# A hybrid decoder layer on one core: the output gate made token-major, two pooling maps to a PSUM bank, token-major weight tiles by high part first, and a norm's columns scaled ahead of its transposes

## The chip, the core and the metric

The kernel runs on one core of one Trainium2 chip. The metric is device time in microseconds (us), from launch to end, of one execution. The core has five engines that run side by side and meet only at semaphores: TensorE (PE; its weight loads are shown apart as PEld), VectorE (DVE), ScalarE (ACT), GpSimd (POOL), and SyncE (SP), which issues most DMAs. PE writes its results to PSUM, which this kernel uses as eight banks of 512 fp32 columns, four of them (`acc`) for the projections; DVE and ACT carry them on to SBUF.

## The reference, cut to what matters

256 tokens of width 2048 pass through one layer. All matrices are fp32.

```
proj = h @ w_in                      # 2048 x 5136: q, k, v, z, b, a, p
o = chunk_gated_delta_rule(q, k, v, g, beta)           # 8 heads x 128
o = o * rsqrt(mean(o*o) + eps) * norm_w                # per head
o_gdn = o * silu(z)                                    # the output gate
pooled = window_means(p) - p                           # 4 groups x 256 channels
o_pool = einsum("btgc,gcd->btgd", pooled, pool_w) * pool_scale   # the pooling maps
h = LN1(ALPHA*h + concat(o_gdn, o_pool) @ w_out)
h = LN2(ALPHA*h + cross_attention(h, mem))             # wq, wk, wv, wo: 2048 x 2048
h = LN3(ALPHA*h + square(relu(h @ w_up)) @ w_down)     # 2048 x 8192, 8192 x 2048
```

## The kernel before, in words

**Products in three parts.** Each fp32 operand is split into a high part (rounded to fp32r by ACT, line 189) and a low part (the difference, by DVE, line 190). A product is the sum of high x high, high x low and low x high. A weight matrix comes in tiles of 256 rows by 512 columns (`W`, 512 KB); the split makes `H` and `L` of each, three buffers of either, so a tile is split two or three tiles ahead of its matmuls.

**Two ways to lay out a projection.** `proj_a` puts out features on the partitions: the weight block is the stationary operand and the tokens stream. In its `wide` form a matmul of 512 columns (line 328) streams the high and the low part of the tokens side by side against a high weight block, and one of 256 columns (line 332) streams the high part against the low block; the two halves of the result are added later (`fold`: ACT copies the bank, line 201, POOL adds the halves, line 204). A tile takes 8 of each. `proj_b` puts out tokens on the partitions (token-major): the tokens are stationary and the weights stream, 512 columns at a time, by three matmuls per row block and token block (`one`, lines 374 to 376: high.H, high.L, low.H). A tile takes 12. `proj_b` serves w_out, w_v, w_o and w_down.

**The order of the work.** The list `plan` holds every weight tile in order, and `run` walks it: it issues the DMAs and the splits of the tiles ahead, then the tile's matmuls, then one step of the background scheduler `bg`. Background tasks (the delta rule, the gate, the pooling, the attention, the norms) are generators; each `yield` names the DVE and ACT time that it spent and how many tiles to wait. `bg.step` takes from them until a slot's budget is spent. So the order on each engine is fixed when the program is built, and each engine runs its queue in that order.

**The places that the change touches.** w_in's tiles for z are projected by wide `proj_a`; `z_evac` folds each head's block and a later step applies SiLU to 128x256 (line 934). `solve` ends by scaling the delta rule's output by its norm (line 916); `gate_out` transposes a head (line 944), multiplies by norm_w and the gate on DVE (line 946) and splits the result. `pool_map` makes a group of four maps: for each, six matmuls of 256 columns (lines 1003 to 1005) into a bank of its own (`acc()` hands out four banks in turn), an ACT eviction with the scale (line 1009) and a DVE eviction of the low part (line 1010). The group stands as one tile in the plan, once inside and once behind w_k's tiles. The second norm works on two token blocks, `norm0` and `norm1`. `Norm.start` centers and scales columns on DVE (lines 1105 and 1110) and hands two groups of 512 columns to ACT and POOL (`beside`); `Norm.turn` transposes blocks on PE (line 1311) and stores them by ACT and DVE (lines 1134 and 1136). The dictionaries `after_o` and `after_up` say behind which tile of w_o and of the first w_up tiles each step stands. The first w_up tiles are walked twice, for either token block (lines 1377 to 1379).

Of the kernel before, what the change touches and what calls it, by code (L numbers as in the profile page):

```python
# [15 lines left out]
P = 128  # L16
T = 256
# [107 lines left out]
def hybrid_layer(ctx: ExitStack, tc: tile.TileContext, xT, xtok, memT, w_ba, w_in, small, w_pool,  # L125
# [19 lines left out]
    def chunk(shape, dtype=F32, late=False):  # L145
        pool = second[0] if late else cp
        return pool.tile([P] + list(shape), dtype, tag="c", name=nm("c"))
# [44 lines left out]
    def pair():  # L192
        a = chunk([2, T], F32R)
        r = Pair((a[:, 0, :], a[:, 1, :]))
        r.wide = a.rearrange("p s c -> p (s c)")
        return r
# [170 lines left out]
    def proj_b(src, acts, evac, resident=False, pre=None, post=None):  # L367
# [3 lines left out]
        def one(t, kt, h, l):  # L371
            a = acts[kt]
            c = slice(t * P, (t + 1) * P)
            mm(out=accs[t], lhsT=a[0][:, c], rhs=h, start=kt == 0, stop=False)  # L374
            mm(out=accs[t], lhsT=a[0][:, c], rhs=l, start=False, stop=False)  # L375
            mm(out=accs[t], lhsT=a[1][:, c], rhs=h, start=False, stop=kt == KT - 1)  # L376
            if kt == KT - 1:
                evac(t, accs[t])

        def both(j):  # L380
            def fn(h, l):
                if j == 0:
                    accs.extend(acc() for _ in range(NT))
                for t in range(NT):
                    for s in range(2):
                        one(t, 2 * j + s, h[:, s, :], l[:, s, :])
            return fn

        def first(j):
# [447 lines left out]
    def solve(g):  # L837
# [73 lines left out]
        r = small_tile([NT, 4])  # L911
        rsqrt(r, ms, [NT, 4])
        yield 1.2, 1.5, 0
        for a in range(NT):
            for i in range(4):
                V.tensor_scalar(out=os_[a][:, i, :], in0=os_[a][:, i, :], scalar1=r[:, a, i:i + 1],
                                scalar2=None, op0=ALU.mult)
                yield .2, 0, 0
        og[g] = os_

    zsil = [None] * 4

    def z_evac(g):
        def evac(n, o):
            h = 4 * g + n
            if h % 2 == 0:
                zsil[h // 2] = chunk([2, T])
            bg.urgent.append(silu(h, fold(o, zsil[h // 2][:, h % 2, :])))
        return evac

    def silu(h, z):
        yield 0, 0, 1
        yield 0, 0, 1
        S.activation(out=z, in_=z, func=AF.Silu)
        bg.event(f"z{h}")
        yield 0, .35, 0

    def gate_out(h):
        g, n = h // 4, h % 4
        zs = zsil[h // 2][:, h % 2, :]  # L940
        yield from free_aux()
        ps = aux()
        for a in range(NT):
            nc.tensor.transpose(out=ps[:, a * P:(a + 1) * P], in_=og[g][a][:, n, :], identity=ident)
        yield 0, 0, 1
        V.scalar_tensor_tensor(out=zs, in0=ps[:, :T], scalar=par[:, C_NW:C_NW + 1], in1=zs,
                               op0=ALU.mult, op1=ALU.mult)
        done()
        yield .4, 0, 1
        mix[8 + h] = pair()  # L950
        split(*mix[8 + h], zs)
        yield .35, .3, 0

    pooled = [None] * 8
    raw_p = {}
# [37 lines left out]
    def pool_map(g):  # L993

        def fn(h, l):
            for gi in range(2):
                for nb in range(2):
                    ps = acc()
                    o = ps[:, :T]
                    for s in range(2):  # L1000
                        a = pooled[4 * g + 2 * gi + s]
                        c = slice(nb * P, (nb + 1) * P)
                        mm(out=o, lhsT=h[:, gi, s, c], rhs=a[0], start=s == 0, stop=False)
                        mm(out=o, lhsT=h[:, gi, s, c], rhs=a[1], start=False, stop=False)
                        mm(out=o, lhsT=l[:, gi, s, c], rhs=a[0], start=False, stop=s == 1)
                    b = 4 * g + 2 * gi + nb
                    m = pair()
                    sc = par[:, C_PS + b:C_PS + b + 1]
                    S.activation(out=m[0], in_=o, func=AF.Copy, scale=sc)
                    V.scalar_tensor_tensor(out=m[1], in0=o, scalar=sc, in1=m[0].bitcast(F32),  # L1010
                                           op0=ALU.mult, op1=ALU.subtract)
                    mix[b] = m
        add("w", w_pool[g], [2, 2, 256], fn, [f"pool{4 * g + i}" for i in range(4)])
# [13 lines left out]
    for g in range(2):  # L1027
        bg.add(f"solve{g}", solve(g), *[f"v{4 * g + i}" for i in range(4)], *[f"diag{q}" for q in range(4)])
    for h in range(HEADS):
        bg.add(f"gate{h}", gate_out(h), f"solve{h // 4}", f"z{h}")  # L1030
    for h in range(HEADS):
        bg.add(f"q{h}", q_head(h), f"x{8 + h}", f"k{h}")
    for h in range(HEADS):
# [5 lines left out]
            t[2] += tuple(f"q{4 * int(t[0][5:]) + i}" for i in range(4))  # L1039
    for i in range(2, 6):  # L1040
        proj_a(w_in[i], xs, conv_evac(4 * i, True), wide=True)
    proj_a(w_in[6], xs, z_evac(0), wide=True)
    proj_a(w_in[7], xs, z_evac(1), wide=True)
    proj_a(w_in[8], xs, p_evac(0), wide=True)
    proj_a(w_in[9], xs, p_evac(1), wide=True)

# [273 lines left out]
    def steps(*fs):  # L1320
# [9 lines left out]
        11: steps((norm0.turn, 0, 1)),  # L1330
        13: steps((norm0.turn, 2, 3)),
        14: steps((norm0.turn, 4, 5)),
        15: steps((norm1.start, 5, [half0, half1, (1, ALL)], [half0, half1], (2, 3))),
    }
    after_up = {
        2: steps((norm1.turn, 0, 1), (norm1.scale, (1, ALL))),
        J: steps((norm1.turn, 2, 3)),
        J + 1: steps((norm0.turn, 6, 7)),
        J + 2: steps((norm1.turn, 4, 5)),
# [241 lines left out]
```

## Time and profile before

| | |
|---|---|
| median of 3 runs | 1483.5 us (1483.07 to 1484.04) |
| the profiled execution | 1483.14 us, of it span 1481.3 us |
| PE busy | 1472.4 us, 99% of the span |
| DVE busy | 943.4 us, 64% |
| ACT busy | 728.2 us, 49% |
| POOL busy | 148.8 us, 10% |
| DMA | 280.45 MB, mean 189 GB/s |

The span runs from the first instruction to the last; 1.8 us lie around it. PE's busy time counts overlapping matmuls: one of 512 columns is shown as 390 ns or so from start to end, while the next may start some 230 ns after it. So the pace of PE is read from starts, not from durations.

### The profile page before, as it was taken

How to read it: one execution, taken by the hardware profiler on the slowest of the kernel's cores; microseconds unless marked ns; L12 is line 12 of the kernel's file. 1: busy time of each engine (PE TensorE's matmuls, PEld its weight loads, DVE VectorE, ACT ScalarE, POOL GpSimd, SP SyncE). 2: the span in 40 equal slices, each digit the busy share in tenths (PEclk: the TensorE clock that was granted, in tenths of full speed). 3: DMA queues.
4: the chain of work that ended last, by engine and by line, in shares of the span. 5: the costliest groups of instructions: out<-in, count | busy, mean ns of one | idle time of the engine just before them, and what ended most of it. 6: DMA issues, size and time to landing. Idle time of an engine off the chain costs nothing.

```text
span 1481.3 us, 21143 instructions
## 1 busy us (share of the span) xinstructions
PE 1472.4 (99%) x8050; PEld 1277.3 (86%) x8050; DVE 943.4 (64%) x1464; ACT 728.2 (49%) x1064; POOL 148.8 (10%) x191
## 2 busy tenths in 40 slices
PE   9999999999999999999999999999999999999998
PEld 9988889899888888998888888888888888888887
DVE  6778976867656755555685555566545565556557
ACT  6765555755533545453545443355344453345442
POOL 1024323700300000000130000000000000000001
PEclk9999999999999999999999999999999999999999
DMA  8556565535865555444735655555656655555562
GB/s 274 182 203 185 171 187 173 194 130 170 288 197 189 183 190 190 155 133 159 276 131 178 199 191 190 196 187 183 198 190 212 222 192 194 196 190 185 194 233 83
DMA packets 86902, 280.45 MB, mean 189 GB/s; under 512 B 13920, under 2 KB 15216, under 8 KB 86800
## 3 DMA queue, kind: packets, MB, share of 16 engines
q1 hardware_dynamic: 79072, 268.73, 54.7%
q0 software_dynamic: 2960, 9.58, 2.0%
q10 hardware_dynamic: 4768, 0.79, 0.3%
q8 instruction: 63, 1.03, 0.3%
q14 instruction: 39, 0.32, 0.1%
HBM read 276.43 MB, written 2.63 MB: 188 GB/s over the span
## 4 chain that ended last, share of the span: by engine, by line
PE 98%; DVE 1%; ACT 0%; issue 0%; DMA 0%; DVEq 0%; ACTq 0%
PE acc L328 30%; PE acc L332 15%; PE acc L374 13%; PE acc L376 13%; PE acc L375 13%; PE acc L349 5%; PE acc L411 0%; PE acc L410 0%; PE acc L409 0%; PE acc L1377 0%; PE acc L1379 0%; PE acc L1378 0%; PE aux L1224 0%; PE aux L1223 0%; PE aux L855 0%
## 5 line engine op out<-in xcount | busy, mean ns | idle before, releaser
L190 DVE TENSOR_TENSOR L<-W,H 128x1024 fp32r<-128x1024 f32 x469 | 578.1, 1234 | 462.2 <-ACT H L189 456.6
L189 ACT ACTIVATE H<-W 128x1024 fp32r<-128x1024 f32 x479 | 507.4, 1059 | 582.7 <-PE acc L376 298.7
L328 PE MATMUL acc<-c,H 128*128 128x512 f32 x1920 | 499.2, 394 | 0.0
L328 PEld LDWEIGHTS acc<-c,H 128*128 128x128 f32 x1920 | 338.3, 189 | 55.3 <-DVE c L190 0.6
L374 PE MATMUL acc<-H,c 128*128 128x512 f32 x832 | 325.2, 391 | 0.0
L376 PE MATMUL acc<-H,c 128*128 128x512 f32 x832 | 323.9, 389 | 0.0
L375 PE MATMUL acc<-L,c 128*128 128x512 f32 x832 | 323.9, 389 | 0.0
L332 PEld LDWEIGHTS acc<-c,L 128*128 128x128 f32 x1920 | 274.2, 190 | 27.2
L332 PE MATMUL acc<-c,L 128*128 128x256 f32 x1920 | 281.3, 282 | 0.0
L376 PEld LDWEIGHTS acc<-H,c 128*128 128x128 f32 x832 | 156.2, 188 | 32.6
L375 PEld LDWEIGHTS acc<-L,c 128*128 128x128 f32 x832 | 156.3, 188 | 31.7
L374 PEld LDWEIGHTS acc<-H,c 128*128 128x128 f32 x832 | 156.2, 188 | 31.7
L204 POOL TENSOR_TENSOR c<-c 128x256 f32<-128x256 f32 x60 | 49.8, 855 | 369.9 <-DVE L L190 186.6
L190 DVE TENSOR_TENSOR c<-c,c 128x256 fp32r<-128x256 f32 (+1 forms) x170 | 76.6, 503 | 11.4 <-ACT c L189 11.4
L189 ACT ACTIVATE c<-c 128x256 fp32r<-128x256 f32 (+1 forms) x170 | 66.6, 456 | 4.6 <-DMA c<-xT 4.6
L349 PE MATMUL acc<-c,H 128*128 128x256 f32 x384 | 66.7, 290 | 0.7 <-ACT H L189 0.7
L1095 POOL DMA_DIRECT2D c<-lnrow x24 | 12.9, 539 | 517.8 <-PE acc L376 345.0
L349 PEld LDWEIGHTS acc<-c,H 128*128 128x128 f32 x384 | 58.2, 198 | 1.6 <-ACT H L189 1.4
L349 PE MATMUL acc<-c,L 128*128 128x256 f32 x192 | 48.0, 289 | 0.0
L201 ACT ACTIVATE c<-acc 128x512 f32<-128x512 f32 x60 | 35.6, 599 | 18.9 <-PE acc L332 14.9
L566 DVE SCALAR_TENSOR_TENSOR c<-c,par 128x255 f32<-128x255 f32 (+2 forms) x72 | 38.2, 538 | 3.6 <-ACT c L563 1.9
L349 PEld LDWEIGHTS acc<-c,L 128*128 128x128 f32 x192 | 34.4, 197 | 0.2 <-DVE L L190 0.2
(258 smaller groups left out, 1000.8 us busy)
## 6 DMA issues: line engine op xcount, KB each, us to landing
W<-w_up SPq DMA_DIRECT2D x127, 512.0 KB, 4.2
W<-w_down SPq DMA_DIRECT2D x120, 512.0 KB, 4.3
W<-w_in SPq DMA_DIRECT2D x76, 512.0 KB, 3.4
W<-w_k SPq DMA_DIRECT2D x32, 512.0 KB, 3.4
W<-w_out SPq DMA_DIRECT2D x32, 512.0 KB, 4.3
W<-w_v SPq DMA_DIRECT2D x32, 512.0 KB, 3.3
W<-w_q SPq DMA_DIRECT2D x32, 512.0 KB, 3.3
W<-w_o SPq DMA_DIRECT2D x24, 512.0 KB, 3.5
```

What stands on the lines that cost most here:

```text
L189: S.activation(out=h, in_=src, func=AF.Copy)
L190: eng.tensor_tensor(out=l, in0=src, in1=h.bitcast(F32), op=ALU.subtract)
L201: S.activation(out=ab.rearrange("p s c -> p (s c)"), in_=o, func=AF.Copy)
L204: nc.gpsimd.tensor_tensor(out=r, in0=ab[:, 0, :], in1=ab[:, 1, :], op=ALU.add)
L328: mm(out=accs[n], lhsT=h[:, s, c], rhs=acts[k0 + s].wide, start=k0 + s == 0, stop=False)
L332: mm(out=accs[n][:, :T], lhsT=l[:, s, c], rhs=acts[k0 + s][0], start=False, stop=k0 + s == KT - 1)
L349: mm(out=accs[n][:, :T], lhsT=w[:, s, n * P:(n + 1) * P], rhs=acts[kt][x], start=kt == 0 and w is h and x == 0, stop=kt == KT - 1 and w is l)
L374: mm(out=accs[t], lhsT=a[0][:, c], rhs=h, start=kt == 0, stop=False)
L375: mm(out=accs[t], lhsT=a[0][:, c], rhs=l, start=False, stop=False)
L376: mm(out=accs[t], lhsT=a[1][:, c], rhs=h, start=False, stop=kt == KT - 1)
L566: V.scalar_tensor_tensor(out=u[:, sh:], in0=x[:, :T - sh], scalar=w[:, 3 - sh:4 - sh], in1=u[:, sh:], op0=ALU.mult, op1=ALU.add)
L1095: nc.gpsimd.dma_start(out=c, in_=lnrow[i:i + 1, g * 512:(g + 1) * 512].partition_broadcast(P))
```

## The change: what it does

Five edits:

1. z's two groups of w_in tiles go through `proj_b`: 12 matmuls of 512 columns per tile. The result stands token-major in a full bank, and one ACT instruction per token block takes it through SiLU. The folds of z fall away.
2. `solve` multiplies by the norm and by the gate in one DVE instruction; `gate_out` only transposes, and evicts the high and the low part straight from PSUM.
3. `proj_b`'s `both` no longer calls `one`: a tile runs all high.H, then all low.H, then all high.L, across both token blocks; in the last tile of a group, block by block.
4. `pool_map` takes one bank for two maps, a half each.
5. `norm1`'s scaling of column group 1 moves from `after_up[2]`, behind the first transposes, to the end of `after_o[15]`, ahead of them.

```
 def both(j): ...
-                for t in range(NT):
-                    for s in range(2):
-                        one(t, 2 * j + s, h[:, s, :], l[:, s, :])
+                last = 2 * j + 2 == KT
+
+                for ts in [[t] for t in range(NT)] if last else [range(NT)]:
+                    for x, w in ((0, h), (1, h), (0, l)):
+                        for t in ts:
+                            for s in range(2):
+                                kt = 2 * j + s
+                                mm(out=accs[t], lhsT=acts[kt][x][:, t * P:(t + 1) * P], rhs=w[:, s, :],
+                                   start=kt == 0 and x == 0 and w is h, stop=kt == KT - 1 and w is l)
+                    if last:
+                        evac(ts[0], accs[ts[0]])
...
+        while f"z{g}" not in bg.done:
+            yield 0, 0, 1
         for a in range(NT):
             for i in range(4):
-                V.tensor_scalar(out=os_[a][:, i, :], in0=os_[a][:, i, :], scalar1=r[:, a, i:i + 1],
-                                scalar2=None, op0=ALU.mult)
+                V.scalar_tensor_tensor(out=os_[a][:, i, :], in0=os_[a][:, i, :], scalar=r[:, a, i:i + 1],
+                                       in1=four(zsil[g][a])[:, i, :], op0=ALU.mult, op1=ALU.mult)
...
     def z_evac(g):
...
+        def evac(t, o):
+            zsil[g][t] = chunk([512])
+            S.activation(out=zsil[g][t], in_=o, func=AF.Silu)
...
     def gate_out(h):
...
-        V.scalar_tensor_tensor(out=zs, in0=ps[:, :T], scalar=par[:, C_NW:C_NW + 1], in1=zs,
-                               op0=ALU.mult, op1=ALU.mult)
+        mix[8 + h] = m = pair()
+        sc = par[:, C_NW:C_NW + 1]
+        S.activation(out=m[0], in_=ps[:, :T], func=AF.Copy, scale=sc)
+        V.scalar_tensor_tensor(out=m[1], in0=ps[:, :T], scalar=sc, in1=m[0].bitcast(F32), op0=ALU.mult,
+                               op1=ALU.subtract)
         done()
-        yield .4, 0, 1
-        mix[8 + h] = pair()
-        split(*mix[8 + h], zs)
-        yield .35, .3, 0
...
     def pool_map(g): ...
             for gi in range(2):
+                ps = acc()
                 for nb in range(2):
-                    ps = acc()
-                    o = ps[:, :T]
+                    o = ps[:, nb * T:(nb + 1) * T]
...
-    proj_a(w_in[6], xs, z_evac(0), wide=True)
-    proj_a(w_in[7], xs, z_evac(1), wide=True)
+    proj_b(w_in[6], xs, z_evac(0))
+    proj_b(w_in[7], xs, z_evac(1))
...
-        15: steps((norm1.start, 5, [half0, half1, (1, ALL)], [half0, half1], (2, 3))),
+        15: steps((norm1.start, 5, [half0, half1, (1, ALL)], [half0, half1], (2, 3)), (norm1.scale, (1, ALL))),
     }
     after_up = {
-        2: steps((norm1.turn, 0, 1), (norm1.scale, (1, ALL))),
+        2: steps((norm1.turn, 0, 1)),
```

How the instructions stand on the engines, at three places.

PE, the first two maps of the first `pool_map`, before (`H` and `L` are the split map weights, `c` the pooled tokens, `acc` the bank; in brackets the engine whose semaphore a row waits for):

```order
L1003 MATMUL acc_3986<-c_3483,H_3911 128x256 [waits Activation_49]
L1004 MATMUL acc_3986<-c_3483,H_3911 128x256
L1005 MATMUL acc_3986<-c_3483,L_3912 128x256
L1003 MATMUL acc_3986<-c_3526,H_3911 128x256
L1004 MATMUL acc_3986<-c_3526,H_3911 128x256
L1005 MATMUL acc_3986<-c_3526,L_3912 128x256
L1003 MATMUL acc_3996<-c_3483,H_3911 128x256 [waits Activation_49]
L1004 MATMUL acc_3996<-c_3483,H_3911 128x256
```

The same place in the change:

```order
L1008 MATMUL acc_3915<-c_3264,H_3826 128x256 [waits Activation_49]
L1009 MATMUL acc_3915<-c_3264,H_3826 128x256
L1010 MATMUL acc_3915<-c_3264,L_3827 128x256 [waits DVE_49]
L1008 MATMUL acc_3915<-c_3419,H_3826 128x256
L1009 MATMUL acc_3915<-c_3419,H_3826 128x256
L1010 MATMUL acc_3915<-c_3419,L_3827 128x256
L1008 MATMUL acc_3915<-c_3264,H_3826 128x256 [waits DVE_49]
L1009 MATMUL acc_3915<-c_3264,H_3826 128x256
```

The second map now writes the bank of the first (`acc_3915`), and its first matmul waits for a DVE semaphore, where it waited for an ACT semaphore before a bank of its own (`acc_3996`); its operands are those that the first map has already read. The third and fourth map, and the second `pool_map`, stand in the same way.

PE, the first tile of z, the change (`H` and `L` of the weights now stream, `c` holds the tokens; before, this was 8 rows of line 328 over four banks and 8 of line 332):

```order
L391 MATMUL acc_1960<-H_1884,c_143 128x512 [waits Activation_49]
L391 MATMUL acc_1960<-H_1884,c_154 128x512
L391 MATMUL acc_1961<-H_1884,c_143 128x512 [waits Activation_49]
L391 MATMUL acc_1961<-H_1884,c_154 128x512
L391 MATMUL acc_1960<-H_1884,c_143 128x512
L391 MATMUL acc_1960<-H_1884,c_154 128x512
L391 MATMUL acc_1961<-H_1884,c_143 128x512
L391 MATMUL acc_1961<-H_1884,c_154 128x512
L391 MATMUL acc_1960<-L_1885,c_143 128x512 [waits Pool_49]
L391 MATMUL acc_1960<-L_1885,c_154 128x512
L391 MATMUL acc_1961<-L_1885,c_143 128x512
L391 MATMUL acc_1961<-L_1885,c_154 128x512
```

This is also the new order of every token-major tile: the four matmuls that read `L` come last, and the bank changes at every second matmul instead of at every sixth.

DVE, the start of `norm1`, before (`c_4474` is column group 1, line 1110 the scaling, line 1136 the store of transposed blocks):

```order
L1110 SCALAR_TENSOR_TENSOR c_4470<-c_4470,t_7883,c_7609 128x256
L1121 SCALAR_TENSOR_TENSOR t_7888<-t_7870,t_7883 128x1
L1136 TENSOR_TENSOR c_7763<-aux_7915,c_7763 128x128 [waits Activation_49]
L1136 TENSOR_TENSOR c_7764<-aux_7915,c_7764 128x128
L1136 TENSOR_TENSOR c_7769<-aux_7918,c_7769 128x128 [waits Activation_49]
L1136 TENSOR_TENSOR c_7770<-aux_7918,c_7770 128x128
L1110 SCALAR_TENSOR_TENSOR c_4474<-c_4474,t_7883,c_7611 128x512
```

and in the change (the lines are 5 higher):

```order
L1115 SCALAR_TENSOR_TENSOR c_4338<-c_4338,t_7775,c_7501 128x256
L1126 SCALAR_TENSOR_TENSOR t_7780<-t_7762,t_7775 128x1
L1115 SCALAR_TENSOR_TENSOR c_4342<-c_4342,t_7775,c_7503 128x512
L1141 TENSOR_TENSOR c_7655<-aux_7808,c_7655 128x128 [waits Activation_49]
L1141 TENSOR_TENSOR c_7656<-aux_7808,c_7656 128x128
L1141 TENSOR_TENSOR c_7661<-aux_7811,c_7661 128x128 [waits Activation_49]
L1141 TENSOR_TENSOR c_7662<-aux_7811,c_7662 128x128
```

The scaling of 512 columns has moved ahead of four stores that wait for ACT.

## Rows read from the trace of the kernel before

**Rows 1.** The page: PE's busy time, and its granted clock in 40 slices.

```profile
PE 1472.4 (99%) x8050; PEld 1277.3 (86%) x8050; DVE 943.4 (64%) x1464; ACT 728.2 (49%) x1064; POOL 148.8 (10%) x191
...
PEclk9999999999999999999999999999999999999999
```

**Rows 2.** Waits of PE: who waited for whom, total us, times, longest.

```profile
PE aux L464 <- DVE warm L426: 1.5, 1, 1.5
PE aux L1506 <- DVE c L1504: 1.2, 1, 1.2
PE aux L1311 <- DVE c L1110: 0.7, 1, 0.7
```

**Rows 3.** Timeline of PE, a wide z tile: start us, us, line, operation, tiles.

```profile
157.58 2.00 PE L328 MATMUL acc<-c,H 128*128 128x512 f32 x8
...
160.37 2.00 PE L328 MATMUL acc<-c,H 128*128 128x512 f32 x8
```

**Rows 4.** The same tile from 158.5 us on, a closer window.

```profile
158.51 1.07 PE L328 MATMUL acc<-c,H 128*128 128x512 f32 x4
159.42 0.40 PE L332 MATMUL acc<-c,L 128*128 128x256 f32 x2
```

**Rows 5.** The chain that ended last, in w_down: start us, us, what.

```profile
1040.14 0.23 PE acc L374
...
1055.78 0.23 PE acc L374
```

**Rows 6.** Busy time by stretch (us, busy per engine, granted clock, DMA).

```profile
157.58:205.65 48.07, 48.07 (x283) 42.36 (x281) 42.62 (x70) 23.95 (x35) 13.27 (x9) 1.00 0.55 175
...
1470.00:1476.00 6.00, 4.79 (x20) 2.71 (x19) 4.07 (x12) 0.90 (x2) 1.14 (x2) 1.00 0.22 68
```

**Rows 7.** Groups of instructions: the folds' additions on POOL.

```profile
L204 POOL TENSOR_TENSOR c<-c 128x256 f32<-128x256 f32 x60 | 49.8, 855 | 369.9 <-DVE L L190 186.6
```

**Rows 8.** Timeline around the first pool_map: ACT, DVE, and PE at the second map.

```profile
345.22 2.69 ACT L201 ACTIVATE c<-acc 128x512 f32<-128x512 f32 x4 [1.43 <-PE acc L332]
...
347.83 0.28 PE L1003 MATMUL acc<-c,H 128*128 128x256 f32 x1
...
348.28 1.06 ACT L189 ACTIVATE H<-W 128x1024 fp32r<-128x1024 f32 x1
...
349.23 1.57 ACT L1009 ACTIVATE c<-acc,par 128x256 fp32r<-128x256 f32 x4
...
349.37 1.23 DVE L190 TENSOR_TENSOR L<-W,H 128x1024 fp32r<-128x1024 f32 x1 [4.33 <-ACT H L189]
...
350.51 1.65 DVE L1010 SCALAR_TENSOR_TENSOR c<-acc,par,c 128x256 fp32r<-128x256 f32 x4
```

**Rows 9.** Timeline around the second pool_map, the same.

```profile
375.06 0.28 PE L1003 MATMUL acc<-c,H 128*128 128x256 f32 x1
...
376.29 1.60 ACT L1009 ACTIVATE c<-acc,par 128x256 fp32r<-128x256 f32 x4
...
376.42 1.22 DVE L190 TENSOR_TENSOR L<-W,H 128x1024 fp32r<-128x1024 f32 x1 [0.18 <-ACT H L189]
...
377.57 1.65 DVE L1010 SCALAR_TENSOR_TENSOR c<-acc,par,c 128x256 fp32r<-128x256 f32 x4
```

**Rows 10.** The two evictions of pool_map by source line: duration ns min/median/max.

```profile
L1009 ACT ACTIVATE c<-acc,par x8: 468/482/503, 349.2 to 377.4; 128x256 fp32r<-128x256 f32 x8
...
L1010 DVE SCALAR_TENSOR_TENSOR c<-acc,par,c x8: 473/474/478, 350.5 to 378.7; 128x256 fp32r<-128x256 f32 x8
```

**Rows 11.** Timeline at the second norm's second transposes, DVE and PE.

```profile
766.99 0.88 DVE L1136 TENSOR_TENSOR c<-aux,c 128x128 fp32r<-128x128 f32 x4 [1.91 <-ACT c L1134]
...
767.79 1.42 DVE L1110 SCALAR_TENSOR_TENSOR c<-c,t,c 128x512 f32<-128x512 f32 x1
...
768.14 0.39 PE L1379 MATMUL acc<-H,c 128*128 128x512 f32 x1
...
769.27 0.66 PE L1311 MATMUL aux<-ident,c 128*128 128x128 f32 x4 [0.75 <-DVE c L1110]
```

More of the change, by code (lines that the diff above doesn't have):

```diff
@@ L913, in solve @@
         yield 1.2, 1.5, 0
+        while f"z{g}" not in bg.done:
+            yield 0, 0, 1
         for a in range(NT):
             for i in range(4):
-                V.tensor_scalar(out=os_[a][:, i, :], in0=os_[a][:, i, :], scalar1=r[:, a, i:i + 1],
-                                scalar2=None, op0=ALU.mult)
-                yield .2, 0, 0
+                V.scalar_tensor_tensor(out=os_[a][:, i, :], in0=os_[a][:, i, :], scalar=r[:, a, i:i + 1],
+                                       in1=four(zsil[g][a])[:, i, :], op0=ALU.mult, op1=ALU.mult)
+                yield .22, 0, 0
         og[g] = os_
-    zsil = [None] * 4
+    zsil = [[None] * NT for _ in range(2)]
     def z_evac(g):
[L924 to L928, printed above, removed]
-        return evac
[L931 to L936, printed above, removed]
+        def evac(t, o):
+            zsil[g][t] = chunk([512])
+            S.activation(out=zsil[g][t], in_=o, func=AF.Silu)
+            bg.charge(0, .65)
+            if t == NT - 1:
+                bg.event(f"z{g}")
+        return evac
     def gate_out(h):
         g, n = h // 4, h % 4
-        zs = zsil[h // 2][:, h % 2, :]
         yield from free_aux()
@@ L945, in gate_out @@
         yield 0, 0, 1
-        V.scalar_tensor_tensor(out=zs, in0=ps[:, :T], scalar=par[:, C_NW:C_NW + 1], in1=zs,
-                               op0=ALU.mult, op1=ALU.mult)
+        mix[8 + h] = m = pair()
[3 more added lines that the diff above has]
+                               op1=ALU.subtract)
         done()
-        yield .4, 0, 1
-        mix[8 + h] = pair()
-        split(*mix[8 + h], zs)
-        yield .35, .3, 0
+        yield .5, .4, 0
     pooled = [None] * 8
@@ L1029, in hybrid_layer @@
     for h in range(HEADS):
-        bg.add(f"gate{h}", gate_out(h), f"solve{h // 4}", f"z{h}")
+        bg.add(f"gate{h}", gate_out(h), f"solve{h // 4}")
     for h in range(HEADS):
```

## The prediction

> **What bounds the kernel now.** I read the page first: PE is busy for 99% of the span, at a granted clock of 1.0 in all 40 slices, the 2.4 GHz level, and no other engine is above 64% [rows 1]. PE's waits come next, because a busy PE can hide gaps: its three longest are 1.5 us at the start, 1.2 us in the tail and 0.7 us ahead of a transpose of the second norm [rows 2]. Together that is 3.4 us of 1481.3. So PE's queue is the bound. An edit changes the time in two ways only: by changing how long PE's instructions take to go through, or by putting a wait into that queue or taking one out. Work saved on DVE, ACT or POOL is worth nothing unless PE waits for it.
>
> Then I read PE's pace from starts. The first wide tile of z begins at 157.58 and the next at 160.37 [rows 3]: 2.79 us per tile. The last four of its eight 512-column matmuls take 159.42 - 158.51 = 0.91 us, 0.2275 each, and with the first four, which follow 256-column ones, the eight take 159.42 - 157.58 = 1.84 us, 0.230 each [rows 3, 4]. In a token-major stretch, two starts of line 374 that are 23 rounds of three matmuls apart lie 1055.78 - 1040.14 = 15.64 us apart [rows 5], 15.64 / 69 = 0.2267 us per matmul.
>
> **Edit 1, z token-major.** 12 matmuls at 0.2267 are 2.72 us, against 2.79: 0.07 us less per tile, 16 tiles, -1.1 us. If the new sequence ran at the 0.230 of the wide tile's eight, a tile would take 2.76 and the gain would be 0.5 us. I take -1.1, because the rows of rows 5 are this very form. The stretch of z is 48.07 us long with PE busy in all of it [rows 6], so there is no wait here to win. The eight folds that fall away free POOL of 8 x 0.855 = 6.8 us [rows 7] and ACT of copies; PE waits for neither, so this counts as nothing. A new wait could come where the next group takes over z's last bank: the SiLU that empties it starts when z's last matmul ends, and the next group needs that bank only after six matmuls, 6 x 0.230 = 1.4 us. A copy of a full bank on ACT takes under 0.7 (four in 2.69 us [rows 8]), so I count nothing and keep 0.5 us for the range.
>
> **Edit 2, the gate.** The solve's scaling keeps its eight instructions per group, and each head's gate loses one DVE instruction. The transposes on PE stay 16; the last eight of them move from behind the second pool_map to ahead of w_k's last tile. DVE and ACT do this beside PE's tiles of w_k, as before: nothing. If that cover were gone, each late eviction would hold PE as the maps' do below.
>
> **Edit 3, high part first.** Every token-major tile outside z keeps its 12 matmuls. No wait for a low part stands among PE's waits [rows 2], so the later reading of `L` wins nothing. Against it could speak that the bank now changes at every second matmul. The wide tile also changes bank after two, and its last four run at 0.2275 [rows 4], which is the token-major pace to within 0.001. So nothing. The bound: there are 208 such tiles (32 of w_out, 32 of w_v, 24 of w_o, 120 of w_down), and if all ran at 0.230, that is 208 x 12 x 0.0033 = +8.2 us; a stretch with other banks at the full pace speaks against it, and I give it 3 in 100.
>
> **Edit 4, two maps to a bank.** This is the term that decides. In the new order the second map's first matmul waits for a DVE semaphore, though its operands have been read before: what it waits for is the DVE eviction of the first map, which reads the same bank. In the kernel before, the second map started at 347.83, right behind the first, while the eviction of the first on DVE began at 350.51 [rows 8] and took 0.474 [rows 10]: it ended at 350.98. Why so late: ACT worked off four fold copies of w_k's last tile (345.22), another copy and the high split of a later tile (348.28) before it came to the first eviction at 349.23; DVE had that tile's low split (349.37, 1.23 us) in front. That queue stands in the same order in the change. So PE stands from 347.83 to 350.98, 3.15 us, plus a release of 0.06 (DVE's scaling in rows 11 ends at 769.21, PE's transpose starts at 769.27): 3.2 us. At the second pool_map the second map started at 375.06 and DVE's first eviction at 377.57 [rows 9]: 377.57 + 0.474 + 0.06 - 375.06 = 3.04; a gate eviction stands there now in place of a split of 256 columns on either engine, about as long, for which I add 0.1: 3.1 us.
>
> The third map has a bank of its own and starts at once; the fourth waits for the third's evictions. By then ACT and DVE have nothing else in front: a 256-column matmul shows 0.28 us from start to end [rows 8], two in a row 0.40 [rows 4], so the next may start after 0.12 and 0.16 of the last remain; then ACT 0.48, DVE 0.474 [rows 10] and three hand-overs of some 0.04 (ACT to DVE 349.34 to 349.37 in rows 8, DVE to PE 0.06 as above): 1.2 us. Two of these. In sum 3.2 + 3.1 + 1.2 + 1.2 = +8.7 us.
>
> Queued behind the waiting matmul is all of PE's queue: the rest of the map, the transposes, and w_k's or w_out's tiles. Nobody gains from the pause, because PE waited for nothing there before, so it is not given back. Low bound: all four waits as short as the last two, 4.9 us. High bound: the long ones grow by one more split in front (1.06 on ACT, 1.23 on DVE [rows 8]), +1.2 each, 11.1 us.
>
> The Trainium skill, PSUM — Partial Sum Buffer, section PSUM bank collisions raise a hardware error, asks that PSUM be guarded by bank and not by address. By it the wait must stand for two halves of one bank, which the order shows; without it the sum would lose the 8.7 us. No row of the kernel before shows two outputs sharing a bank in this way.
>
> **Edit 5, the scaling ahead of the transposes.** PE's matmul of 768.14 would have been followed 0.23 us later; the transposes start at 769.27, 0.75 us idle by the view and 0.90 by starts, held by the scaling of column group 1, which DVE began at 767.79 behind its stores [rows 11]. In the new order it runs in the 1.91 us in which DVE idled ahead of those stores [rows 11]: 1.42 us fit even at that length. So the wait goes: -0.9 us. What is late next: the stores of these transposes keep their distance from PE, so nothing. Bounds: 0, if the stores come later by it, and -0.9.
>
> **The sum.** -1.1 + 8.7 - 0.9 = +6.7 us. The profiled execution took 1483.14 us, span 1481.3; the median of the runs is 1483.5. 1483.14 + 6.7 = 1489.8; by the median 1490.2. I say 1490.
>
> **The rivals.**
> - *The shared bank costs nothing* (not slower): the second map's evictions are early enough, or the wait is met when PE gets there. Then -1.1 - 0.9 = -2.0: 1481.1 to 1481.5, within 0.2%. For it speaks only that PE waited for almost nothing before; against it 350.51 against 347.83 [rows 8]. It would need the first eviction to end within 0.1 us of the first map, and ACT's eviction alone takes 0.48. Chance 0.05; 0.02 of that for gains that I have not seen and that carry it beyond 0.2%.
> - *Four short waits*: the new background order leaves ACT and DVE idle ahead of the maps, so the long waits shrink to 1.2. Then 4.9 - 2.0 = +2.9, 1486.2, at the edge of 0.2%. The fold copies and the tile's split stand in front in the new order too. Chance 0.08.
> - *The clock falls*: PE now stands for about 3 us twice, longer than any wait before; in the longest stretch of waits, 1470 to 1476, the granted clock stayed at 1.00 with PE idle for 1.2 us of it [rows 6]. At 1.2 GHz a token-major tile takes another 2.7 us; with one such tile's worth behind each long wait, +5.4: 1495.4. The Trainium skill, TensorE: Matmul & The Clock Gate, Part 1, has PE return to the lower level after it has been idle; no run here shows it, since no idle time of PE in this trace is that long. Chance 0.06.
> - *Token-major tiles slower in the new order* (edit 3's bound): +6.7 + 8.2, 1498. Chance 0.03.
>
> **How the numbers follow.** The forecast has 0.78. Its own range, with 4.9 to 11.1 for the maps narrowed to +-2.5 around 8.7, 0.6 for z and 0.9 for the norm, is 1487 to 1493.5. For 8 in 10 I reach down to the four short waits and up to 1493.5: 1486 to 1493.5. Within 0.2% (3.0 us, about what a measurement of this kernel tells from no change) lie the first rival and two thirds of the second, 0.03 + 0.05, and some of the forecast's low end, 0.04: 0.12. Faster 0.02. Slower 0.86.
>
> **What the changed profile would show.** PE's waits should have a new group, maps (line 1008) held by DVE's line 1015, four times, about 8.7 us in sum, the longest about 3.2. The wait of the transposes for the scaling should be gone. z's tiles should start 2.72 us apart, with the 512-column matmuls of line 391 0.227 apart in w_down too. I am wrong if PE runs from the first to the second map without a pause, if the pauses are all near 1.2 us, or if PE's granted clock shows a slice below 9.

## The result, and the profile after

The change took 1494.24 us, the median of six runs (1488.47 to 1498.1), against 1483.28 for the kernel before (six runs, 1483.07 to 1484.04): a ratio of 1.0072, interval 1.0056 to 1.0089. It is slower, as forecast, but by 11 us instead of 6.7, above the range. The runs are unusually far apart, and 1494.24 lies half-way between two of them (1492.41 and 1496.07). The same kernel, run again beside other kernels, took 1491.32 (1490.06 to 1498.31, six runs). Sorted by the clock that PE was granted on average over the span (1.000 is full speed, 2.4 GHz), the twelve runs fall into three groups:

| mean granted clock | times, us |
|---|---|
| 1.000 | 1488.47, 1490.06, 1490.07, 1490.14, 1490.18 |
| 0.996 | 1492.41, 1492.47 |
| 0.993 | 1496.01, 1496.07, 1498.07, 1498.10, 1498.31 |

The kernel before has a clock of 1.0 in every slice [rows 1]. The profiled execution of the change is one of the second group: 1492.41 us, span 1490.7. The page of the change, the rows that answer to [rows 1]: PE's count fell by 64, its busy time grew, and one slice of the clock shows an 8.

```profile
PE 1473.3 (99%) x7986; PEld 1275.6 (86%) x7986; DVE 950.6 (64%) x1456; ACT 724.4 (49%) x1052; POOL 139.8 (9%) x183
...
PEclk9999999998999999999999999999999999999999
```

Waits of PE in the change (total us, times, longest), which answer to [rows 2]. The maps' four waits are new, and so is the length of the solve's wait, line 863 (0.3 before, line 855). The norm's wait of [rows 2] is gone.

```profile
PE acc L1008 <- DVE c L1015: 8.2, 4, 3.1
PE aux L472 <- DVE warm L434: 1.5, 1, 1.5
PE aux L1511 <- DVE c L1509: 1.2, 1, 1.2
PE aux L863 <- DVE c L857: 1.1, 1, 1.1
```

The solve's wait in the kernel before:

```profile
PE aux L855 <- DVE c L849: 0.3, 1, 0.3
```

Timeline of PE in the change, two tiles of z, against [rows 3]. The pace is 161.16 - 158.44 = 2.72 us a tile.

```profile
158.44 1.98 PE L391 MATMUL acc<-H,c 128*128 128x512 f32 x8
160.25 1.07 PE L391 MATMUL acc<-L,c 128*128 128x512 f32 x4
161.16 1.98 PE L391 MATMUL acc<-H,c 128*128 128x512 f32 x8
```

Timeline of DVE and of PE in the change around the first `pool_map`, against [rows 8]. DVE has the low split of a later tile in front (349.05) and reaches the first map's eviction at 350.19; PE's second map starts behind it at 350.72. DVE had stood idle for 5.50 us ahead of that split, which waits for ACT's high split: so the order of the queues makes the eviction late, not DVE's load.

```profile
349.05 1.23 DVE L190 TENSOR_TENSOR L<-W,H 128x1024 fp32r<-128x1024 f32 x1 [5.50 <-ACT H L189]
350.19 0.48 DVE L1015 SCALAR_TENSOR_TENSOR c<-acc,par,c 128x256 fp32r<-128x256 f32 x1
...
350.72 0.58 PE L1008 MATMUL acc<-c,H 128*128 128x256 f32 x1 [3.06 <-DVE c L1015]
...
353.23 0.41 PE L1010 MATMUL acc<-c,L 128*128 128x256 f32 x1
354.73 0.58 PE L1008 MATMUL acc<-c,H 128*128 128x256 f32 x1 [1.08 <-DVE c L1015]
...
356.18 3.61 PE L328 MATMUL acc<-c,H 128*128 128x512 f32 x8
```

The last line is what the forecast's sum lacks: eight matmuls of 512 columns take 3.61 us where [rows 3] has 2.00. Busy time by stretch of the change (us, then busy per engine, granted clock, DMA) shows the clock: 1.00 for the first 2.1 us of PE's wait, then, from 349.8 on, 0.50, the 1.2 GHz level, for 10.2 us, of them the last 0.9 us of the wait.

```profile
347.00:349.80 2.80, 0.66 (x6) 0.45 (x4) 0.75 (x1) 2.38 (x4) 1.39 (x3) 1.00 0.00 0
349.80:360.00 10.20, 8.20 (x28) 7.13 (x29) 4.50 (x9) 4.43 (x11) 0.00 (x0) 0.50 0.16 51
360.00:365.00 5.00, 5.00 (x31) 4.39 (x30) 4.16 (x14) 1.96 (x2) 0.00 (x0) 1.00 0.63 200
```

The second run of the change (span 1488.5) was profiled in an execution in which the clock stayed up. Its waits are the same, yet the tile behind the maps takes its 2.02. Timeline of PE there:

```profile
348.17 0.28 PE L1008 MATMUL acc<-c,H 128*128 128x256 f32 x1
...
352.11 0.39 PE L1008 MATMUL acc<-c,H 128*128 128x256 f32 x1 [3.06 <-DVE c L1015]
...
354.88 0.39 PE L1008 MATMUL acc<-c,H 128*128 128x256 f32 x1 [1.08 <-DVE c L1015]
...
355.69 2.02 PE L328 MATMUL acc<-c,H 128*128 128x512 f32 x8
...
378.91 0.28 PE L1008 MATMUL acc<-c,H 128*128 128x256 f32 x1
```

From the first map group to the second, this execution takes 378.91 - 348.17 = 30.74 us. In the first profile the same rows stand at 346.79 and 381.16, 34.37 apart; 0.14 of the difference is a longer wait, and 3.5 us are the lower clock.

So my theory was: at full clock the change costs what was forecast, and each group of waits can bring PE down to 1.2 GHz for a while, which costs some 3.5 us more. Rivals: the new order of edits 1 to 3 slows PE or the clock by itself; or the runs merely scatter.

### The profile page after: what moved, and what is told of

Same layout as the page of the kernel before. It is cut to its first block, busy times and chain, and to the rows that moved or that the text cites. A ratio compares the mean times of both kernels' runs of the same rounds, so it can differ in the third digit from the quotient of the medians.

```text
span 1490.7 us, 21002 instructions
## 1 busy us (share of the span) xinstructions
PE 1473.3 (99%) x7986; PEld 1275.6 (86%) x7986; DVE 950.6 (64%) x1456; ACT 724.4 (49%) x1052; POOL 139.8 (9%) x183
## 4 chain that ended last, share of the span: by engine, by line
PE 98%; DVE 1%; ACT 0%; DMA 0%; issue 0%; SPq 0%; DVEq 0%
PE acc L391 41%; PE acc L328 28%; PE acc L332 14%; PE acc L349 4%; PE acc L419 1%; PE acc L417 1%; PE acc L418 1%; PE acc L1382 1%; PE acc L1384 0%; PE acc L1383 0%; PE acc L376 0%; PE acc L375 0%; PE acc L374 0%; DVE L L190 0%; DMA c<-w_in 0%; PE aux L1229 0%
## 5 line engine op out<-in xcount | busy, mean ns | idle before, releaser
L328 PE MATMUL acc<-c,H 128*128 128x512 f32 x1792 | 467.2, 395 | 0.1
L391 PE MATMUL acc<-H,c 128*128 128x512 f32 x1792 | 449.2, 390 | 0.0
L391 PEld LDWEIGHTS acc<-H,c 128*128 128x128 f32 x1792 | 334.5, 188 | 68.2
L328 PEld LDWEIGHTS acc<-c,H 128*128 128x128 f32 x1792 | 317.3, 189 | 51.5 <-DVE c L190 0.5
L332 PEld LDWEIGHTS acc<-c,L 128*128 128x128 f32 x1792 | 256.3, 190 | 25.5
L332 PE MATMUL acc<-c,L 128*128 128x256 f32 x1792 | 262.8, 282 | 0.0
L391 PE MATMUL acc<-L,c 128*128 128x512 f32 x896 | 244.1, 389 | 0.0
L391 PEld LDWEIGHTS acc<-L,c 128*128 128x128 f32 x896 | 168.2, 188 | 35.0
L349 PEld LDWEIGHTS acc<-c,H 128*128 128x128 f32 x384 | 56.5, 192 | 2.0 <-ACT H L189 1.8
L349 PE MATMUL acc<-c,L 128*128 128x256 f32 x192 | 47.2, 284 | 0.0
L190 POOL TENSOR_TENSOR L<-W,H 128x1024 fp32r<-128x1024 f32 x10 | 25.4, 2539 | 97.2 <-ACT H L189 97.2
L218 ACT ACTIVATE c<-acc 128x256 f32<-128x256 f32 x60 | 23.0, 384 | 23.0 <-PE acc L332 23.0
L349 PEld LDWEIGHTS acc<-c,L 128*128 128x128 f32 x192 | 33.6, 192 | 0.2 <-DVE L L190 0.2
```

What stands on the lines that cost most here:

```text
L190: eng.tensor_tensor(out=l, in0=src, in1=h.bitcast(F32), op=ALU.subtract)
L218: S.activation(out=r, in_=o[:, :T], func=AF.Copy)
L328: mm(out=accs[n], lhsT=h[:, s, c], rhs=acts[k0 + s].wide, start=k0 + s == 0, stop=False)
L332: mm(out=accs[n][:, :T], lhsT=l[:, s, c], rhs=acts[k0 + s][0], start=False, stop=k0 + s == KT - 1)
L349: mm(out=accs[n][:, :T], lhsT=w[:, s, n * P:(n + 1) * P], rhs=acts[kt][x], start=kt == 0 and w is h and x == 0, stop=kt == KT - 1 and w is l)
L391: mm(out=accs[t], lhsT=acts[kt][x][:, t * P:(t + 1) * P], rhs=w[:, s, :], start=kt == 0 and x == 0 and w is h, stop=kt == KT - 1 and w is l)
```

## The experiments

Each kernel was timed beside the kernel before on the same chip; ratios are to that. The mean clock covers the whole span, and in most profiles the clock also falls in the last microseconds, behind PE's last matmul: in the profile of edits 1 and 2 alone it is at 0.50 from 1481.3 to the end at 1483.7, which by itself makes the mean 0.999. So 0.999 is no sign of a fall in mid-stream; where I speak of one, a profile or a lower mean shows it.

**Banks of its own for each map, all else of the change kept.**

```diff
-                ps = acc()
                 for nb in range(2):
-                    o = ps[:, nb * T:(nb + 1) * T]
+                    ps = acc()
+                    o = ps[:, :T]
```

> The change without edit 4: every pooling map has a bank of its own again. Theory (the shared bank costs four waits, about 8.2 us, and these bring the lower clock): both go, the granted clock is 1.000 in every run, and the time is that of before less 1.1 (z) and 0.9 (norm), plus the 0.8 by which the solve's wait for its subtraction grew: 1481 to 1482.5, with runs within 1 us. Rival (the loss or the spread comes from another edit, such as the new order of the token-major tiles): above 1485, or runs that differ by several us with clocks under 1.000.

Measured: 1483.34 (1481.92 to 1484.51, 11 runs), ratio 1.0000 (0.9992 to 1.0009), the clock at 0.999 to 1.000 in every run. So the shared bank brings the whole loss and the fall of the clock with it. But the time is above the expected 1481 to 1482.5: nearly all of the 2 us that edits 1 and 5 should have won is missing. Waits of PE in this kernel:

```profile
PE aux L863 <- DVE c L857: 1.1, 1, 1.1
PE acc L328 <- DVE c L1015: 0.9, 1, 0.9
PE acc L391 <- DVE c L1015: 0.8, 1, 0.8
```

Two of them are new: the first weight tile behind either map group. Timeline of PE there, in this kernel: the tile follows the last map and takes over a bank that the first maps have just filled.

```profile
349.64 0.28 PE L1010 MATMUL acc<-c,L 128*128 128x256 f32 x1
350.82 2.12 PE L328 MATMUL acc<-c,H 128*128 128x512 f32 x8 [0.91 <-DVE c L1015]
```

In the kernel before, the same stretch of PE's timeline has matmuls of the delta rule (lines 892 and 893) and transposes of the gate (line 944) between the two, from 349.99 on; the tile starts 1.92 us later and waits for nothing. Behind the second group stood eight transposes of the gate, from 377.22 on.

```profile
349.99 0.39 PE L892 MATMUL aux<-c,c 128*128 128x128 f32 x2
...
351.78 0.38 PE L944 MATMUL aux<-ident,c 128*128 128x128 f32 x2
351.91 2.09 PE L328 MATMUL acc<-c,H 128*128 128x512 f32 x8
```

**Only edit 4, in the kernel before.**

```diff
             for gi in range(2):
+                ps = acc()
                 for nb in range(2):
-                    ps = acc()
-                    o = ps[:, :T]
+                    o = ps[:, nb * T:(nb + 1) * T]
```

> The kernel before with edit 4 alone. Theory: four waits of the maps for VectorE, 8 to 9 us in sum, so 1491.5 to 1492.5 in runs at clock 1.000 and 3 to 8 us more in runs whose mean clock is lower. Rival (the waits matter only together with the moved background work): under 1486.

Measured: 1497.27 (1495.77 to 1499.16, 4 runs), ratio 1.0094 (1.0081 to 1.0108), clock 0.994 to 0.997 in all four. Against the kernel before on this chip (1483.44) that is +13.8: 8.7 for the waits as forecast, which leaves some 5 for the clock. Its profile has the four waits, here among PE's waits:

```profile
PE acc L1003 <- DVE c L1010: 8.1, 4, 3.1
```

And its busy time by stretch has the lower clock behind the long waits of both map groups, for 3.4 us from 351.5 on and for 6.8 from 385.6 on:

```profile
350.00:351.40 1.40, 0.00 (x0) 0.00 (x0) 1.40 (x2) 0.26 (x1) 0.00 (x0) 1.00 0.00 0
351.40:354.80 3.40, 2.93 (x12) 2.64 (x12) 0.63 (x2) 0.70 (x2) 0.00 (x0) 0.51 0.50 154
...
386.00:392.00 6.00, 4.92 (x20) 4.43 (x20) 2.61 (x5) 3.11 (x8) 2.22 (x5) 0.50 0.93 301
```

None of the other edits is in this kernel, so the rival that only they pull the clock down falls.

**Work in the waits.** If the clock falls because PE stands, matmuls of no use in the waits should keep it up, though they can't shorten the waits. `keep_warm` issues matmuls on zeros, into a bank that nothing reads.

```diff
                     o = ps[:, nb * T:(nb + 1) * T]
+                    if nb:
+                        keep_warm(2 if gi else 7)
```

> The change with matmuls on zeros (256 columns, 0.43 us each, into a spare bank, their result unused) put ahead of the waiting maps: seven in the first and two in the second wait of each group. They take no longer than the wait. Theory (TensorE's idle time brings the lower clock, and that makes the spread of the runs): the evictions come as before, so the time is that of the change at full clock, 1488 to 1490, in every run, with mean clock 1.000. Rival (the lower clock or the spread has another cause): runs from 1488 to 1498 as for the change.

Measured: 1491.49 (1491.17 to 1491.68, 5 runs), ratio 1.0054 (1.0042 to 1.0067), clock 0.999 to 1.000, and the runs lie within 0.5 us. The time is above what was expected. In the first group the fillers end with the wait, which has 3.2 us as in the change. In the second the first filler itself waits for its bank, and the pause by starts grows from 3.10 to 383.86 - 379.78 - 0.12 = 3.96 us. Timeline of PE there:

```profile
379.78 0.28 PE L1012 MATMUL acc<-c,L 128*128 128x256 f32 x1
380.92 3.29 PE L472 MATMUL aux<-warm 128*128 128x256 f32 x14 [0.86 <-DVE c L954]
383.86 0.47 PE L1010 MATMUL acc<-c,H 128*128 128x256 f32 x1
```

A second kernel with fewer:

```diff
-                        keep_warm(2 if gi else 7)
+                        keep_warm(1 if gi else 5)
```

> As the filler before, with five matmuls on zeros in the long wait and one in the short wait of a group, so that they end before the evictions do. Theory (the shared bank alone costs some 8.9 us, what comes on top in the change is the lower clock): 1488.5 to 1490 with clock 0.999 to 1.000 and runs within 1 us. Rival (the fillers themselves cost the time): lower by the two fillers' length per group or the same spread as the change.

Measured: 1490.58 (1489.08 to 1491.04, 5 runs), ratio 1.0049 (1.0036 to 1.0061), clock 1.000 in all five; a little above the expected interval. The fillers are not the reason: one still waits for its bank, but the pause is 383.35 - 380.13 - 0.12 = 3.10 us, and the four pauses sum to 8.8 as in the change at the full clock. The profiled execution has a span of 1489.1, 0.6 above the second profile of the change, and it reaches its first map 0.64 us later, at 348.81 instead of 348.17: the difference stands ahead of the maps. Timeline of PE in this kernel:

```profile
348.81 0.28 PE L1010 MATMUL acc<-c,H 128*128 128x256 f32 x1
...
380.13 0.28 PE L1012 MATMUL acc<-c,L 128*128 128x256 f32 x1
381.27 2.43 PE L472 MATMUL aux<-warm 128*128 128x256 f32 x10 [0.86 <-DVE c L954]
383.35 0.46 PE L1010 MATMUL acc<-c,H 128*128 128x256 f32 x1
```

In ten runs out of ten the mean clock was 0.999 to 1.000, neither profile has a fall at the maps, and no time was above 1491.7, where seven of twelve runs of the change were. The evictions come as late as before, and only PE's idle time is filled: so that idle time brings the fall, and mere scatter is out. What makes the fall come in one execution and not in the next stays open.

**Two shared banks filled in turn.** The first halves of both banks come before the second halves, so each group waits once instead of twice.

```diff
-            for gi in range(2):
-                ps = acc()
-                for nb in range(2):
+            banks2 = [acc(), acc()]
+            for nb in range(2):
+                for gi in range(2):
+                    ps = banks2[gi]
```

> The change with the maps in another order: the first halves of both banks, then the second halves. Theory: a group then waits once, for the first eviction, 0.7 us less than the long wait of the change, about 2.5 us, and the second halves' other wait is met: 4.9 us in sum instead of 8.2 to 8.9, so 1485 to 1487 at clock 1.000. If the lower clock comes by the length of the wait, fewer runs than four of six show it; if it comes at any such pause, as many. Rival (the number of shared banks, not the wait, sets the loss): as the change, 1488 and above at clock 1.000.

Measured: 1488.05 (1486.89 to 1488.82, 7 runs), ratio 1.0032 (1.0021 to 1.0044). The time is above the 1485 to 1487 expected for the full clock. The waits are as expected, 2.35 and 2.23 us by the view, 4.9 by starts; the rest is the clock, 0.998 in six runs and 0.999 in the profiled one. There it falls behind the first wait, 1.3 us after PE has resumed, for 3.4 us from 352.7 on, and not behind the second. So a wait of 2.35 us can be followed by a fall, and the reading that a longer wait makes it more frequent is not borne out: all seven runs show one (six by a mean of 0.998, the seventh in its profile), against seven of twelve of the change. The rival's 1488 was for clock 1.000, and the waits, 4.6 us by the view instead of 8.2, speak against it. Why the fall is shorter here than the change's 10.2 us stays open. Timeline of PE in this kernel, the first group's wait and the tile behind the maps:

```profile
351.35 0.38 PE L1009 MATMUL acc<-c,H 128*128 128x256 f32 x1 [2.35 <-DVE c L1016]
...
353.03 2.33 PE L328 MATMUL acc<-c,H 128*128 128x512 f32 x5
```

Busy time by stretch there:

```profile
350.00:352.20 2.20, 0.85 (x7) 0.85 (x8) 1.69 (x3) 0.38 (x2) 0.00 (x0) 1.00 0.16 30
352.20:355.60 3.40, 3.40 (x15) 2.82 (x14) 1.89 (x5) 2.81 (x7) 0.00 (x0) 0.57 0.34 135
```

**Sharing in the first group alone.**

```diff
-                ps = acc()
+                shared = acc() if g == 0 else None
                 for nb in range(2):
-                    o = ps[:, nb * T:(nb + 1) * T]
+                    ps = shared or acc()
+                    o = ps[:, (nb if shared else 0) * T:][:, :T]
```

> The change with shared banks in the first group of maps alone. Theory (each group costs its two waits, 4.4 to 4.6 us, and on top what the lower clock takes behind them, as a separate price that varies from run to run): own banks' 1483.3 less 1.1 plus 4.6, so 1486.8 at clock 1.000, and up to 5 us more in runs with a lower clock; the middle half-way between own banks and the change. Rival (the lower clock needs both groups): 1486 to 1488 in all runs.

Measured: 1488.79 (1485.15 to 1491.1, 11 runs), ratio 1.0034 (1.0024 to 1.0044). The runs split in two: five at clock 1.000 with 1485.15 to 1487.76 (mean 1486.4), six at 0.996 with 1488.79 to 1491.1 (mean 1490.6). One fall therefore costs some 4.2 us, and comes in about half of the executions of one program. The profile is of an execution at 1.000, so the fall in the six others is read from their mean clock, which is that of the change's first profile.

**The other edits alone, in the kernel before.** Edits 1 and 2, with the change's `solve`, `z_evac` and `gate_out`:

```diff
-    proj_a(w_in[6], xs, z_evac(0), wide=True)
-    proj_a(w_in[7], xs, z_evac(1), wide=True)
+    proj_b(w_in[6], xs, z_evac(0))
+    proj_b(w_in[7], xs, z_evac(1))
```

> The kernel before with edits 1 and 2 alone (z token-major and the gate; maps, tile order and norm as before). Theory (these edits save 1.1 us in z's stage but move the background work so that new waits appear: the solve's transposed subtraction +0.8, and the first tiles behind each group of maps, which take over a bank just filled, +0.9 to +1.1 each): about 1.1 less and 2.8 more, so 1484 to 1486, clock 1.000. Rival (the edits only save): 1482.5 or less.

Measured: 1484.2 (1482.71 to 1485.87, 11 runs), ratio 1.0010 (1.0000 to 1.0019). The gain of z is in it (from z's first matmul to the next group 204.57 - 157.57 = 47.00 us, 48.07 before [rows 6]), and still the kernel gains nothing. Its waits:

```profile
PE aux L855 <- DVE c L849: 1.1, 1, 1.1
PE acc L328 <- DVE c L1007: 0.9, 1, 0.9
PE acc L374 <- DVE c L1007: 0.8, 1, 0.8
```

They are those of the kernel with own banks: the new gate has moved the background work that lay behind the maps, and a solve step that had 0.3 us of wait has 1.1. They sum to 2.8, 2.5 more than before.

Edit 3:

```diff
-                for t in range(NT):
-                    for s in range(2):
-                        one(t, 2 * j + s, h[:, s, :], l[:, s, :])
+                last = 2 * j + 2 == KT
+                for ts in [[t] for t in range(NT)] if last else [range(NT)]:
+                    for x, w in ((0, h), (1, h), (0, l)):
+                        for t in ts:
+                            for s in range(2):
...
```

> The kernel before with edit 3 alone (a token-major tile's matmuls by high part first). Theory (the pace of 0.2267 us per matmul depends neither on the order of banks nor on weights that are loaded twice, and no low part was waited for): the time of before, within 0.7 us. Rival (changing bank at every second matmul runs at the 0.230 of a wide tile's eight): +8 us.

Measured: 1483.5 (1481.14 to 1484.15, 11 runs), ratio 0.9999 (0.9990 to 1.0007): nothing.

Edit 5:

```diff
-        15: steps((norm1.start, 5, [half0, half1, (1, ALL)], [half0, half1], (2, 3))),
+        15: steps((norm1.start, 5, [half0, half1, (1, ALL)], [half0, half1], (2, 3)), (norm1.scale, (1, ALL))),
...
-        2: steps((norm1.turn, 0, 1), (norm1.scale, (1, ALL))),
+        2: steps((norm1.turn, 0, 1)),
```

> The kernel before with edit 5 alone (column group 1 of the second norm scaled ahead of the first transposes). Theory: the wait of 0.9 us goes and none takes its place: 1482.0 to 1483.0, and the profile shows no wait of the norm's transposes above 0.3 us. Rival (the stores behind it come later and hold the next tile): the time of before.

Measured: 1482.18 (1481.09 to 1483.91, 11 runs), ratio 0.9995 (0.9987 to 1.0004): 1.1 us less by the medians, the interval still reaches 1. In its timeline of PE the transposes that stood at 769.27 [rows 11] follow the matmul ahead of them after 0.23 us:

```profile
768.84 0.39 PE L1379 MATMUL acc<-H,c 128*128 128x512 f32 x1
769.07 0.60 PE L1311 MATMUL aux<-ident,c 128*128 128x128 f32 x4
```

The longest wait in mid-stream of this execution stands at a place that the edit doesn't touch:

```profile
PE aux L613 <- ACT c L606: 1.4, 1, 1.4
```

**A version to win with.** The change with a bank for each map, the second half of the maps in `aux` banks so that the next tile finds its banks free, and one tile more between the solve's steps.

```diff
-                yield .6, 0, 0
+                yield .6, 0, 1
...
-                ps = acc()
                 for nb in range(2):
-                    o = ps[:, nb * T:(nb + 1) * T]
+                    ps = psum.tile([P, 512], F32, tag="aux", name=nm("acc"), bufs=AUXB) if gi else acc()
+                    o = ps[:, :T]
```

> The change with own banks for the maps, two of a group's four in banks of the other four that the projections don't use (aux), so that the next tile finds its banks long empty; and one tile more between the solve's subtraction and the matmuls that read it. Theory (with own banks the change only equals the kernel before because three new waits of 1.3, 1.1 and 0.9 us eat its gains): these waits go, so 1480 to 1481.5 and faster than before by 0.15 to 0.2%. Rival (the gains of z and of the norm are not there, or the bank waits move on to the background's transposes): 1483 and above.

Measured: 1484.03 (1482.58 to 1484.59, 11 runs), ratio 1.0001 (0.9992 to 1.0010): missed. The three waits are gone, but the last map of the second group now waits for an `aux` bank, and in the profiled execution the clock falls behind it, 0.8 us after PE has resumed (mean 0.998; of the eleven runs eight have 0.998 and three 0.999). The eight matmuls of the next tile start over 382.14 - 378.74 = 3.40 us instead of 1.84 [rows 3, 4]. So 1.9 + 1.6 us come in for the 2.8 that went, +0.7 on own banks' 1483.34. PE's timeline in this kernel:

```profile
377.91 0.39 PE L1008 MATMUL acc<-c,H 128*128 128x256 f32 x1 [1.88 <-DVE c L1015]
...
378.74 3.57 PE L391 MATMUL acc<-H,c 128*128 128x512 f32 x8
382.14 1.09 PE L391 MATMUL acc<-L,c 128*128 128x512 f32 x4
```

Busy time by stretch there:

```profile
378.00:381.40 3.40, 3.40 (x13) 2.82 (x14) 1.66 (x4) 2.42 (x6) 2.21 (x5) 0.60 0.99 335
```

**The change once more**, for its scatter (the table above).

> The change itself, beside the others on this chip: 1488.5 to 1490 in runs at clock 1.000, and the more the lower the mean clock, up to 1498 at 0.993. A mean clock of 0.993 over 1495 us is 1495 x 0.007 x 2 = 21 us at the lower of two levels, so about 10 us lost; the runs should lie near 1488.5 plus 1495 x (1 - clock).

Measured: 1491.32 (1490.06 to 1498.31, 6 runs), ratio 1.0060 (1.0042 to 1.0077). No version tried beats the kernel before beyond the measurement; edit 5 alone comes nearest.

## Why the prediction was right or wrong

**The bound, right.** PE's queue decides: POOL's busy time fell by 9 us and DVE's rose by 7 against [rows 1], and the time follows neither; each wait put into PE's queue came out in it.

**Edit 4's waits, right to 0.3 us.** Forecast 3.2, 1.2, 3.1 and 1.2, in sum 8.7. By starts, less the pace of 0.12 of a 256-column matmul, the first profile has 350.72 - 347.38 - 0.12 = 3.22 and 354.73 - 353.23 - 0.12 = 1.38, and the second group 3.10 and 1.24: 8.94. The one at 1.38 was met at the lower clock; at the full clock it is 1.24 and the sum 8.8. The cause is as named: the eviction on DVE behind a tile's low split, which waits for ACT.

**The step that failed: the clock.** The rival *the clock falls* was told with its place and mechanism and given 0.06, and the sum was made at the full clock. The reason given for so low a chance was that the clock had stayed at 1.00 in the stretch from 1470 to 1476 with 1.2 us of idle time in it [rows 6]. That row reaches no wait of 3 us; the step treated a wait without precedent in the trace as if the nearest one spoke for it. The runs showed a fall in seven of the change's twelve executions and in all four with edit 4 alone; the sign that the prediction itself named, a slice of the clock below 9, is in the first profile. The rival's price was low too: 2.7 us for each fall, by one tile at half pace; measured 3.5, in a stretch of 10.2 us (the two profiles of the change), and 4.2 (the two groups of runs of one shared group). With both falls, 1490 + 2 x 3.5 to 2 x 4.2 = 1497 to 1498.4, where the runs at 0.993 lie (1496.0 to 1498.3). That those have a fall behind both map groups is worked out, not seen: two stretches of 10.2 us at half clock are 10.2 of 1497 lost, a mean of 0.993. At full clock the forecast holds: five runs, 1488.47 to 1490.18, against 1490. How far the median of six lies from it hangs on how many of the six have a fall, four in the first set and three in the second (1491.32): that part is chance, the missing term is not.

**Edit 1, right in its term, wrong in what it leaves behind.** The tile takes 2.72 us, 0.07 less than before, as summed. No wait came at z's last bank. But edits 1 and 2 together were to cost nothing beside it, since the cover was said to stay. The solve's wait grew by 0.8, which is in the change's time; and behind the maps the cover went away, the case that the text named and didn't price. In the change these last waits don't show, because the shared bank has PE stand earlier; with own banks they cost 0.9 + 0.8 by the view.

**Edit 3, right:** nothing (ratio 0.9999 alone). **Edit 5, right:** the wait is gone, and the stores behind it hold nobody.

**The sum at full clock.** The second profile has a span of 1488.5, +7.2 on 1481.3, where 6.7 was forecast. Its terms: the launch -0.5 (z's first matmul stands at 157.07 instead of 157.58 [rows 3], with only the start ahead of it that either kernel has), z -1.1, the solve +0.8, the maps +8.8, the norm -0.9: +7.1. That the forecast is met within 0.5 us is in part luck: the solve's +0.8 was not in it, and the start, which scatters by more than that, gives 0.5 back. In the first profile the launch gives -1.9 and the lower clock +3.5, the rest is alike: 9.3 of 9.4.

## What to carry to other kernels

When PE is busy without a break at the full clock, a wait put into its queue can have two prices: its length, and a lower clock behind it (in these profiles after waits of 1.9 us and more, not after those of up to 1.4); where the trace of before has no wait so long, the second price belongs into the sum or the range, not into a small rival. In this kernel two outputs in one bank make PE wait for both evictions of the first, and the length of that wait is read from what stands ahead of these evictions on ACT and DVE. Work that follows such a group is cover for the evictions; an edit that moves background work away from there uncovers them, even if its own work costs nothing.

## What the hardware showed that I had not expected

- A wait of 1.9 us (spare `aux` banks) and one of 2.35 (two banks in turn) inside a full stream of matmuls were followed by a granted clock of 0.5 for 3.4 us, waits of 3.1 by one for 3.4 and 6.8 (edit 4 alone) and 10.2 us (the change), though PE worked again behind them. In the profiles of the kernels whose waits in mid-stream stay at or under 1.4 us (own banks, the gate, the order or the norm alone) the clock is at 1.00 up to the last microseconds, and their mean was 0.999 to 1.000 in every run. Whether the length of the wait alone decides is not shown.
- The same program, with the same waits, had the fall in some executions and not in others. The Trainium skill, TensorE: Matmul & The Clock Gate, Part 1, has the chip judge PE's activity in a rhythm that isn't tied to the kernel's start; that the falls come and go from run to run fits this, though no run here tests it. The same section of the Trainium skill has the lower level come back through idling; here idle times of 1.9 us amid dense work were enough.
- Two executions of the change reach z's first matmul at 155.69 and 157.07 us, with the same program ahead of it: 1.4 us of the scatter lies in the start.
